# A two-layer feed-forward: weight sums behind the adds to h, squares and norm one job later, the last operand pair on VectorE

## The chip, the core and the metric

The kernel runs on one core of one Trainium2 chip. A core has a matrix engine (TensorE, "PE" in the profile), three engines for elementwise work (VectorE "DVE", ScalarE "ACT", GpSimd "POOL"), a queue that mainly issues transfers (SyncE "SP"), and DMA engines that move data between the device memory and the on-chip memory. Each engine runs its own instruction list in order and waits on semaphores for the others. The metric is the device time of one execution, in microseconds (us).

## The reference

The program computes two transformer blocks one after the other. The part that the change touches is the feed-forward of the second block, which occurs twice, once per layer:

```python
def _swiglu(h, w_gu, w_down):
    gate, up = jnp.split(h @ w_gu, 2, axis=-1)
    return (jax.nn.silu(gate) * up) @ w_down

for layer in range(DEPTH_2):              # 2 layers
    h = h + mixer(_rmsnorm(h, ...))       # even layer: recurrence and attention, odd: retention
    h = h + _swiglu(_rmsnorm(h, ffn_norm[layer]), ffn_w_gu[layer], ffn_w_down[layer])
```

`h` has 1024 features, held as eight tiles of 128 features (`hT`, index f). The norm divides each token by the root of the mean of its squared features. The kernel multiplies the raw, gain-scaled h by the weights and applies the norm's factor R to the product afterwards, so the products need not wait for the norm, but the silu does.

## The kernel before

**Numbers in two parts.** Every operand of a product is held as a high part (`whi`, `xo0`: a rounded copy, made by ScalarE) and a low part (`wlo`, `xo1`: the remainder, a subtraction on VectorE). One step of a product is three matmuls: high by high, high weights by low operand, low weights by high operand.

**Seven products per job.** The gate and up halves of one column tile of 128 are made together by a Strassen-Winograd scheme (class `Wino`). A "job" has seven products of four steps each (k = 0 to 3), `prod`, line 1853: A with `wa`, Bb with `w31`, C with `wa`, A with `w24`, the "fourth" product of the job before (`hhi`, `hlo`), Bb with `w24`, A with `w31`. A job thus has 28 steps; job 0 has no job before it and has 24. The letters A, Bb, C stand for banks of the matmul result memory; A alternates between banks 0 and 1, so job 2 writes the bank that job 0's A used.

**Weights.** `wa` is loaded as it is. `w31` is a sum of two blocks that the DMA engines form (a load by SyncE, then an accumulating load issued by GpSimd, line 1877). `w24` needs two additions on VectorE (lines 1913 and 1915, tile `s`) once that sum has landed. Each is then cast (`whi`) and subtracted (`wlo`, line 1891).

**Operands.** The mixer's last stage adds its output product to `hT` tile by tile in the order of `FORDER` (0, 4, 1, 5, 2, 6, 3, 7), lines 2533 and 2682. Behind each add, ScalarE scales the tile (`hid`, line 2167) and squares it (line 2172), GpSimd adds the square to a running sum (line 2173), and for each pair f, f+4 the seven operands j = 0 to 6 of step k are formed (`operands`): four differences `tt`, two on GpSimd (lines 1836, 1840) and two on VectorE (1838, 1841), and three splits into high and low parts (ScalarE line 296, VectorE line 299).

**Norm and result of a job.** In job 0, between A with `w24` and what follows, TensorE sums the squares over the partitions (line 2194), ScalarE takes the root, VectorE the reciprocal (line 2196). Then `put` finishes a job: GpSimd multiplies gate and up by R (2204), ScalarE takes silu (2206), GpSimd multiplies by R again (2208), VectorE multiplies gate and up, reading bank A (2212, 2213), and the product is split for the down product. `put` is a generator: `tick()` between the products advances the weights and the puts that are under way.

**What sets the order.** Up to job 0 a scheduler orders the instructions of each engine other than TensorE; from job 1 on `manual_schedule` keeps the order in which the code is written on all of them. `keep_in_program_order` pins one instruction, `issue_after` keeps what it holds behind a given instruction.

## Time and profile before

| what | value |
|---|---|
| median of 3 runs | 2330.43 us (2324.12 to 2332.87) |
| profiled execution | 2328.22 us |
| its span, first to last instruction | 2326.4 us |
| TensorE busy | 2164.4 us, 93% of the span |
| VectorE / ScalarE / GpSimd busy | 67% / 48% / 36% |
| job 0 of layer 0, with the norm's matmuls | 1149.86 to 1175.65 us |
| job 0 of layer 1, the same | 1962.86 to 1987.60 us |

The table is read as one execution: durations come from the profiled one, whose span lies 1.8 us below its own time. "Granted clock" (PEclk) is the share of TensorE's full speed that the chip allowed. Its two levels show as 1.00 and about half of that; a stretch in which both occur shows a number between them.

### The profile page before, as it was taken

The numbers are of one execution on the slowest core, as the hardware profiler recorded it, in microseconds if no ns is written. First come the engines' busy times: TensorE is split into PE (matmuls) and PEld (weight loads), VectorE is DVE, ScalarE is ACT, GpSimd is POOL, SyncE is SP. The second block draws the span as 40 slices with busy tenths as digits, with TensorE's granted clock in tenths as the row PEclk, the third lists the DMA queues.
The fourth block names the chain that finished last, engine by engine and source line by source line (L and its number), as shares of the span: only waits on it lengthen the run. The fifth ranks groups of instructions, "written<-read, shape, count | busy, mean of one in ns | idle before, by whom it ended". The sixth has DMA issues, their size and how long they took to land.

```text
span 2326.4 us, 34274 instructions
## 1 busy us (share of the span) xinstructions
PE 2164.4 (93%) x13208; PEld 1874.0 (81%) x13208; DVE 1561.5 (67%) x2146; ACT 1113.8 (48%) x1685; POOL 844.2 (36%) x564
## 2 busy tenths in 40 slices
PE   7789989987999988988899999999999998999999
PEld 1577768756777766877899999988888877999999
DVE  5764886547885876476897594665545556876864
ACT  4313654335876863656554352434323344544432
POOL 2325123234775653641444251422101213542522
PEclk9889989997999998988999999999999999999999
DMA  7564120485997861200366464322222224555642
GB/s 258 181 228 128 42 96 28 175 306 203 334 349 286 302 251 44 78 23 28 103 166 172 121 178 111 99 96 72 78 94 90 73 73 127 147 176 129 181 123 82
DMA packets 112544, 339.09 MB, mean 146 GB/s; under 512 B 14280, under 2 KB 17624, under 8 KB 112374
## 3 DMA queue, kind: packets, MB, share of 16 engines
q1 hardware_dynamic: 91168, 288.85, 36.4%
q0 software_dynamic: 11536, 31.75, 7.2%
q10 hardware_dynamic: 9670, 16.25, 2.2%
q8 instruction: 105, 1.72, 0.3%
q14 instruction: 65, 0.53, 0.1%
HBM read 326.18 MB, written 19.47 MB: 149 GB/s over the span
## 4 chain that ended last, share of the span: by engine, by line
PE 49%; DVE 6%; ACT 2%; issue 2%; POOL 2%; DMA 1%; DVEq 0%; POOLq 0%; ACTq 0%
PE p L1853 17%; PE p L1798 11%; PE p L2070 11%; PE p L2614 3%; PE p L2654 1%; DMA raw<-in_gu 1%; DVE wlo L299 1%; PE p L2617 1%; DVE xo L299 1%; DVE rv L2621 0%; PE p L2488 0%; POOL xt L1741 0%; PE gu L1637 0%; PE p L2458 0%; DVE wloF L1891 0%
## 5 line engine op out<-in xcount | busy, mean ns | idle before, releaser
L296 ACT CAST whi<-raw 128x1024 fp32r<-128x1024 f32 (+1 forms) x237 | 240.0, 1022 | 281.6 <-PE p L1798 120.0
L299 DVE TENSOR_TENSOR wlo<-raw,whi 128x1024 fp32r<-128x1024 f32 (+1 forms) x178 | 254.2, 1447 | 84.1 <-ACT whi L296 80.5
L1853 PE MATMUL p<-xo,whi 128*128 128x264 f32 (+1 forms) x1216 | 225.2, 284 | 18.6 <-ACT xo L296 8.7
L1798 PE MATMUL p<-x,whi 128*128 128x264 f32 (+1 forms) x992 | 230.1, 336 | 3.9 <-DVE xt L2343 1.9
L299 POOL TENSOR_TENSOR wlo<-raw,whi 128x1024 fp32r<-128x1024 f32 x59 | 153.7, 2612 | 189.6 <-ACT whi L296 161.6
L1853 PEld LDWEIGHTS p<-xo,whi 128*128 128x128 f32 x1216 | 188.5, 189 | 20.7 <-ACT xo L296 9.3
L1798 PEld LDWEIGHTS p<-x,whi 128*128 128x128 f32 x992 | 162.8, 194 | 26.1 <-issue 2.6
L1853 PE MATMUL p<-xo,wlo 128*128 128x264 f32 (+1 forms) x608 | 172.5, 284 | 1.2 <-DVE wlo L1891 1.2
L1853 PE MATMUL p<-xo,whiF 128*128 128x264 f32 (+1 forms) x896 | 170.8, 289 | 0.4 <-DVE hT L2682 0.4
L2070 PE MATMUL p<-hid,whi 128*128 128x264 f32 (+1 forms) x928 | 149.5, 283 | 0.0
L1798 PE MATMUL p<-x,wlo 128*128 128x264 f32 (+1 forms) x496 | 144.6, 336 | 0.9 <-DVE wlo L299 0.9
L1853 PEld LDWEIGHTS p<-xo,whiF 128*128 128x128 f32 x896 | 142.9, 194 | 1.1 <-DVE hT L2682 0.7
L1853 PE MATMUL p<-xo,wloF 128*128 128x264 f32 (+1 forms) x448 | 129.2, 288 | 0.0
L2070 PEld LDWEIGHTS p<-hid,whi 128*128 128x128 f32 x928 | 126.7, 188 | 0.2
L2080 DVE TENSOR_TENSOR hT<-hT,p 128x264 f32<-128x264 f32 (+1 forms) x96 | 36.5, 421 | 130.1 <-PE p L2070 130.1
L1360 PE MATMUL gu<-wlo,xh 128*128 128x512 f32 x272 | 110.6, 407 | 12.7 <-DVE wlo L299 7.4
L1853 PEld LDWEIGHTS p<-xo,wlo 128*128 128x128 f32 x608 | 115.1, 189 | 1.4 <-DVE wlo L1891 1.4
L1359 PE MATMUL gu<-whi,xh 128*128 128x512 f32 x272 | 112.1, 412 | 0.0
L1361 PE MATMUL gu<-whi,xlo 128*128 128x512 f32 x272 | 109.5, 402 | 1.8 <-DVE xlo L299 1.8
L1891 DVE TENSOR_TENSOR wlo<-raw,whi 128x1024 fp32r<-128x1024 f32 (+1 forms) x66 | 99.7, 1515 | 2.4 <-ACT whi L1927 1.0
L1798 PEld LDWEIGHTS p<-x,wlo 128*128 128x128 f32 x496 | 86.6, 193 | 10.2 <-issue 1.3
L2070 PE MATMUL p<-hid,wlo 128*128 128x264 f32 (+1 forms) x464 | 93.2, 282 | 0.0
(1317 smaller groups left out, 6044.8 us busy)
## 6 DMA issues: line engine op xcount, KB each, us to landing
raw<-in_moe SPq DMA_DIRECT2D x115, 512.0 KB, 6.1
raw<-in_gu SPq DMA_DIRECT2D x66, 512.0 KB, 4.6
sp<-in_moe SPq DMA_DIRECT2D x48, 512.0 KB, 6.4
raw<-in_gu POOLq DMA_DIRECT2D x44, 512.0 KB, 5.7
mixAB<-in_ada SPq DMA_DIRECT2D x32, 512.0 KB, 4.5
raw<-in_down SPq DMA_DIRECT2D x24, 512.0 KB, 5.9
rawF<-in_gu SPq DMA_DIRECT2D x22, 512.0 KB, 3.5
a<-in_gu SPq DMA_DIRECT2D x44, 256.0 KB, 2.7
```

The source lines that it names most:

```text
L296: i = nc.scalar.copy(hi, src)
L299: self.last = i, (lo_eng or nc.vector).tensor_tensor(lo, src, hi.bitcast(F32), op=ALU.subtract)
L1359: T_.matmul(acc, xh[:, k], hi[:, w], start=k == 0, stop=False)
L1360: T_.matmul(acc, xh[:, k], lo[:, w], start=False, stop=False)
L1361: T_.matmul(acc, xl[:, k], hi[:, w], start=False, stop=k == 7)
L1798: nc.tensor.matmul(a[:, :c1 - c0], w[wi][:, ks], x[xi][:, k, c0 - o:c1 - o], start=k == 0 and wi == 0 and xi == 0, stop=k == nk - 1 and wi ...
L1853: T_.matmul(bank[:, :W], w[wi][:, 512 * i + 128 * k:512 * i + 128 * k + 128], xo[xi][:, k, W * j:W * j + W], start=first and k == 0 and wi ...
L1891: lo = lambda w, src, n=1024: V.tensor_tensor(w[1][:, :n], src, w[0][:, :n].bitcast(F32), op=ALU.subtract)
L2070: nc.tensor.matmul(a_[:, :W], w[wi][:, ks], put.hid[xi][:, k, W * j:W * j + W], start=k == 0 and wi == 0 and xi == 0, stop=k == nk - 1 and ...
L2080: V.tensor_tensor(self.hT[:, f, c0:c1], self.hT[:, f, c0:c1], a_[:, :W], op=ALU.add)
L2614: T_.matmul(acc[t], x[xi][:, kk, ts_], w[wi][:, ws], start=kk == 0 and xi == 0 and wi == 0, stop=kk == 7 and xi == 1)
L2617: T_.matmul(acc[4][:96], xm[:, kk], w[wi][:, ws], start=kk == 0 and wi == 0, stop=kk == 7 and wi == 1)
```

## The change

Four things are edited. (1) In job 0, `w31` is made before `w24`; `w24`'s sums are issued behind the add of h tile f = 3, and job 1's `wa` and `w24` behind the last split of the operands. (2) The squares of the last six h tiles and their sums on GpSimd leave the operand stage and become a generator (`squares`) that the ticks of jobs 0 and 1 advance; the norm stands in job 1 rather than job 0, and job 0's `put` is started after it. (3) The two differences of the last pair that stood on GpSimd go to VectorE, and its four differences are split in two pieces. (4) Job 0 takes its first products in the order A, C, Bb, with bank 6 for C.

```diff
-    def operands(self, xg, f, xo):
+    def operands(self, xg, f, xo, near=False):
...
-        V, G = nc.vector, nc.gpsimd
+        V, G = nc.vector, nc.vector if near else nc.gpsimd
...
+        flat = tt.rearrange("p a n -> p (a n)")
+        if near:
+            b.split(part(0, 3, 5), part(1, 3, 5), flat[:, :2 * W])
         G.tensor_tensor(tt[:, 2], b22, b12, op=ALU.subtract)
         V.scalar_tensor_tensor(tt[:, 3], tt[:, 1], -1.0, b21, op0=ALU.mult, op1=ALU.subtract)
-        b.split(part(0, 3, 7), part(1, 3, 7), tt.rearrange("p a n -> p (a n)"))
+        n = 2 if near else 0
+        b.split(part(0, 3 + n, 7), part(1, 3 + n, 7), flat[:, n * W:])
...
-        lo = lambda w, src, n=1024: V.tensor_tensor(w[1][:, :n], src, w[0][:, :n].bitcast(F32), op=ALU.subtract)
+        lo = lambda w, src, n=1024: self.pin(V.tensor_tensor(w[1][:, :n], src, w[0][:, :n].bitcast(F32), op=ALU.subtract))
...
-            S_.copy(w[0], rs)
+            self.pin(S_.copy(w[0], rs))
...
-            w = self.pair()
-            yield w, s24_(w, ra, rs, i)
-            w = self.pair()
-            yield w, s31_(w, rs, i + 1)
+            s24, s31 = lambda w: s24_(w, ra, rs, i), lambda w: s31_(w, rs, i + 1)
+            for how in (s31, s24) if first else (s24, s31):
+                w = self.pair()
+                yield w, how(w)
+            first = False
...
-        self.make(3)
+        with B.tc.issue_after(B.added):
+            self.make(1)
+        with B.tc.issue_after(self.behind[0]), B.tc.issue_after(self.behind[1]):
+            self.make(2)
+        self.steps.append(self.squares)
         for i in range(2):
             self.half()
-        self.late = 5
+        self.late, self.pin = 5, B.tc.keep_in_program_order
...
-            wa, w24, w31 = have[:3]
-            A, Bb, C = self.A(), self.Bb(), self.C()
-            three = (A, wa, 0, 0), (Bb, w31, 1, 3), (C, wa, 1, 1)
+            A, Bb = self.A(), self.Bb()
             if i == 0:
-                for p_ in three:
-                    self.prod(*p_, ks=range(3))
+                wa, w31, w24 = have[:3]
+                C = B.bank(6)
+                three = (A, wa, 0, 0), (Bb, w31, 1, 3), (C, wa, 1, 1)
+                for p_ in (0, 2, 1):
+                    self.prod(*three[p_], ks=range(3))
+            else:
+                wa, w24, w31 = have[:3]
+                C = self.C()
+                three = (A, wa, 0, 0), (Bb, w31, 1, 3), (C, wa, 1, 1)
...
             self.prod(A, w24, 0, 4, False)
             add(g[:, 0], p1, C)
-            if i == 0:
+            if i == 1:
                 norm()
+                self.steps.append(first)
...
             pend = A, ready, u, p5
-            self.steps.append(put(g, u, A, ready))
+            p_ = put(g, u, A, ready)
+            if i:
+                self.steps.append(p_)
+            else:
+                first = p_
...
-        for f in FORDER:
-            hf = b.hT[:, f, o0:o0 + 2 * W]
-            S_.activation(xg[:, f], hf, AF.Copy, scale=gain[:, f:f + 1])
-            if f == 0:
-                S_.activation(a, hf, AF.Square)
-            else:
-                s = B.tmp(0)[:, :2 * W]
-                S_.activation(s, hf, AF.Square)
-                G.tensor_tensor(a, a, s, op=ALU.add)
+
+        def square(f, pin=False):
+            hf = b.hT[:, f, o0:o0 + 2 * W]
+            s = a if f == 0 else B.tmp(0)[:, :2 * W]
+            i = S_.activation(s, hf, AF.Square)
+            if pin:
+                tc.keep_in_program_order(i)
+            if f:
+                G.tensor_tensor(a, a, s, op=ALU.add)
+
+        def squares():
+            for f in FORDER[2:]:
+                square(f, True)
+                yield
+        for i, f in enumerate(FORDER):
+            S_.activation(xg[:, f], b.hT[:, f, o0:o0 + 2 * W], AF.Copy, scale=gain[:, f:f + 1])
             if f < 4:
-                gens[f] = wn.operands(xg, f, xo)
+                gens[f] = wn.operands(xg, f, xo, i == 6)
             next(gens[f % 4])
+            if i < 2:
+                square(f)
+        wn.behind = [i.ins for i in b.last]
+        wn.squares = squares()
...
 -                nc.vector.tensor_tensor(b.hT[:, f, a0:a1], b.hT[:, f, a0:a1], a[:, :a1 - a0], op=ALU.add)
+                i = nc.vector.tensor_tensor(b.hT[:, f, a0:a1], b.hT[:, f, a0:a1], a[:, :a1 - a0], op=ALU.add)
+            if f == FORDER[6]:
+                B.added = i.ins
```

The last hunk stands at the add to h in the first mixer; the second mixer's add (line 2682) is edited alike.

**VectorE, opening of layer 0's feed-forward.** The rows begin with the split of h tile 2 in both; `s` is the sum for `w24`, `wloF` with number 2583 belongs to `w24` before and to `w31` after; `hT` is the add to h (two pieces per tile). Before:

```order
L299 TENSOR_TENSOR xo_2575_11775<-hid_2573_11773,xo_2574_11774 128x264
L1913 TENSOR_TENSOR s_2584_11792<-raw_11778,rawF_11776 128x512
L1838 SCALAR_TENSOR_TENSOR tt_11845<-tt_11845,hid_2573_11773 128x264
L1915 TENSOR_TENSOR s_2584_11792<-s_2584_11792,rawF_11776 128x512
L1841 SCALAR_TENSOR_TENSOR tt_11845<-tt_11845,hid_2573_11773 128x264
L2533 TENSOR_TENSOR hT_9255<-hT_9255,p_2566_11705 128x264
L2533 TENSOR_TENSOR hT_9255<-hT_9255,p_2567_11706 128x264
L299 TENSOR_TENSOR xo_2575_11775<-hid_2573_11773,xo_2574_11774 128x528
L1891 TENSOR_TENSOR wlo_11886<-raw_11778,whi_11885 128x1024
L1891 TENSOR_TENSOR wloF_2583_11791<-s_2584_11792,whiF_2582_11790 128x1024
L2533 TENSOR_TENSOR hT_9255<-hT_9255,p_2571_11739 128x264
L2533 TENSOR_TENSOR hT_9255<-hT_9255,p_2572_11740 128x264
```

After:

```order
L299 TENSOR_TENSOR xo_2575_11775<-hid_2573_11773,xo_2574_11774 128x264
L2564 TENSOR_TENSOR hT_9255<-hT_9255,p_2561_11671 128x264
L2564 TENSOR_TENSOR hT_9255<-hT_9255,p_2562_11672 128x264
L1895 TENSOR_TENSOR wloF_2583_11791<-raw_11778,whiF_2582_11790 128x1024
L2564 TENSOR_TENSOR hT_9255<-hT_9255,p_2566_11705 128x264
L2564 TENSOR_TENSOR hT_9255<-hT_9255,p_2567_11706 128x264
L1838 SCALAR_TENSOR_TENSOR tt_11831<-tt_11831,hid_2573_11773 128x264
L299 TENSOR_TENSOR xo_2575_11775<-hid_2573_11773,xo_2574_11774 128x528
L1844 SCALAR_TENSOR_TENSOR tt_11831<-tt_11831,hid_2573_11773 128x264
L299 TENSOR_TENSOR xo_2575_11775<-hid_2573_11773,xo_2574_11774 128x264
L1836 TENSOR_TENSOR tt_11844<-hid_2573_11773 128x264
L2564 TENSOR_TENSOR hT_9255<-hT_9255,p_2571_11739 128x264
```

The two additions for `w24` and a low part have left the stretch, the low part of `w31` stands in front of the add of tile 3, and one difference of the last pair (L1836) has come to VectorE.

**ScalarE, end of job 0 and start of job 1 of layer 0.** `whi`/`whiF` are casts of weights (L1919 and L1923 `w24`, L1927 and L1931 `w31`), L2189 the moved squares, `xR` the roots. Before:

```order
L296 CAST xo_2574_11774<-tt_11864 128x1056
L1919 CAST whi_11896<-s_2606_11898 128x1024
L2099 COPY p_2614_11913<-p_2619_11918 128x264
L2102 COPY p_2615_11914<-p_2620_11919 128x264
L1927 CAST whiF_2622_11959<-raw_11782 128x1024
L2113 COPY u_2616_11915<-p_2619_11918 128x264
L2195 ACT_TABLE_LOAD
L2195 ACTIVATE xR_11884<-p_2624_11974,eps_60 128x264
L2195 ACTIVATE xR_11884<-p_2625_11975,eps_60 128x264
L1989 CAST hhi_11907<-a_2608_11905 128x512
L1989 CAST hhi_11911<-a_2611_11909 128x512
```

After:

```order
L2129 COPY u_2610_11899<-p_2613_11902 128x264
L1994 CAST hhi_11891<-a_2602_11889 128x512
L1923 CAST whi_11880<-s_2600_11882 128x1024
L2189 ACTIVATE xt_2616_11935<-hT_9255 128x528
L2189 ACTIVATE xt_2617_11942<-hT_9255 128x528
L1994 CAST hhi_11895<-a_2605_11893 128x512
L2189 ACTIVATE xt_2618_11949<-hT_9255 128x528
L2189 ACTIVATE xt_2621_11967<-hT_9255 128x528
L1931 CAST whiF_2619_11952<-raw_11782 128x1024
L2189 ACTIVATE xt_2622_11974<-hT_9255 128x528
L2189 ACTIVATE xt_2624_11992<-hT_9255 128x528
L1905 CAST whiF_2625_11997<-rawF_11869 128x1024
```

The cast of job 1's `w31` (`whiF` from `raw_11782`) now stands behind four of the moved squares. The tile `xt` that a square writes has two buffers, so the third and the fourth each wait for the sum two before it.

**VectorE, from the reciprocal to the first instruction that reads job 0's bank.** `rg` and `ru` are gate and up of a job, L2212 and L2243 the first instruction of `put` that reads bank A of job 0. Before, in job 0 and job 1:

```order
L2029 TENSOR_TENSOR rg__2617_11916<-p_2614_11913,p_2621_11920 128x264
L1891 TENSOR_TENSOR wloF_2623_11960<-raw_11782,whiF_2622_11959 128x1024
L2029 TENSOR_TENSOR rg__2617_11916<-u_2616_11915,p_2620_11919 128x264
L2196 RECIPROCAL xR_11884<-xR_11884 128x528
L2029 TENSOR_TENSOR ru__2618_11917<-p_2615_11914,p_2619_11918 128x264
L1913 TENSOR_TENSOR s_2639_12043<-raw_11889,rawF_11795 128x512
L1915 TENSOR_TENSOR s_2639_12043<-s_2639_12043,rawF_11795 128x512
L1891 TENSOR_TENSOR wloF_2628_12003<-rawF_11795,whiF_2627_12002 128x1024
L2029 TENSOR_TENSOR rg__2634_12025<-p_2631_12022,p_2638_12029 128x264
L1891 TENSOR_TENSOR wlo_12019<-s_2639_12043,whi_12018 128x1024
L2212 SCALAR_TENSOR_TENSOR ru__2618_11917<-p_2619_11918,rg__2617_11916 128x264
L2213 SCALAR_TENSOR_TENSOR ru__2618_11917<-ru__2618_11917,rg__2617_11916 128x264
```

After, in job 1 and the start of job 2:

```order
L2034 TENSOR_TENSOR ru__2612_11901<-p_2609_11898,p_2613_11902 128x264
L1917 TENSOR_TENSOR s_2637_12038<-raw_11871,rawF_11869 128x512
L1919 TENSOR_TENSOR s_2637_12038<-s_2637_12038,rawF_11869 128x512
L1895 TENSOR_TENSOR wloF_2620_11953<-raw_11782,whiF_2619_11952 128x1024
L1895 TENSOR_TENSOR wloF_2626_11998<-rawF_11869,whiF_2625_11997 128x1024
L2034 TENSOR_TENSOR rg__2632_12020<-p_2629_12017,p_2636_12024 128x264
L2227 RECIPROCAL xR_11863<-xR_11863 128x528
L1895 TENSOR_TENSOR wlo_12014<-s_2637_12038,whi_12013 128x1024
L1895 TENSOR_TENSOR wlo_12072<-raw_11871,whi_12071 128x1024
L2034 TENSOR_TENSOR rg__2632_12020<-u_2631_12019,p_2635_12023 128x264
L2243 SCALAR_TENSOR_TENSOR ru__2612_11901<-p_2613_11902,rg__2611_11900 128x264
L2244 SCALAR_TENSOR_TENSOR ru__2612_11901<-ru__2612_11901,rg__2611_11900 128x264
```

The reciprocal stands one job later, and with it the instruction that reads bank A of job 0; the first matmul of job 2, which writes that bank, waits for it in both kernels.

## Rows read from the trace of the kernel before

**Rows 1.** Page, part 1: busy time, share of the span and instructions per engine.
```profile
PE 2164.4 (93%) x13208; PEld 1874.0 (81%) x13208; DVE 1561.5 (67%) x2146; ACT 1113.8 (48%) x1685; POOL 844.2 (36%) x564
```

**Rows 2.** Windows: stretch, then busy time per engine, PEclk, DMA share.
```profile
1149.86:1175.65 25.79, 15.63 (x79) 13.97 (x77) 21.41 (x25) 15.24 (x22) 11.10 (x9) 0.74 0.55 150
1175.65:1185.87 10.22, 10.22 (x86) 10.22 (x85) 10.19 (x10) 5.60 (x9) 5.31 (x5) 1.00 0.38 82
...
1962.86:1987.60 24.74, 14.79 (x78) 13.34 (x76) 13.67 (x16) 11.64 (x19) 8.03 (x7) 0.66 0.43 113
1987.60:1997.50 9.90, 9.90 (x87) 9.90 (x86) 9.87 (x10) 5.23 (x9) 4.33 (x4) 1.00 0.31 56
```

**Rows 3.** Waits of TensorE, job 0 of layer 0: total, times, longest (us).
```profile
PE p L1853 <- ACT xo L296: 4.0, 1, 4.0
PE p L1853 <- ACT whiF L1919: 2.7, 1, 2.7
PE p L1853 <- DVE xo L299: 2.3, 2, 1.5
```

**Rows 4.** Timeline, TensorE, job 0 of layer 0: start, us, line, op, tiles.
```profile
1153.85 0.48 PE L1853 MATMUL p<-xo,whi 128*128 128x264 f32 x2 [2.72 <-ACT whiF L1919]
...
1169.20 0.65 PE L1853 MATMUL p<-xo,whiF 128*128 128x264 f32 x2
...
1171.18 1.71 PE L2194 MATMUL p<-xt,ones 128*128 128x264 f32 x4
...
1172.53 0.59 PE L1853 MATMUL p<-xo,whiF 128*128 128x264 f32 x2
```

**Rows 5.** Timeline, VectorE, around job 0 of layer 0.
```profile
1149.38 1.24 DVE L1913 TENSOR_TENSOR s<-raw,rawF 128x512 f32<-128x512 f32 x1
...
1152.95 0.76 DVE L2533 TENSOR_TENSOR hT<-hT,p 128x264 f32<-128x264 f32 x2
...
1155.38 1.21 DVE L1891 TENSOR_TENSOR wloF<-s,whiF 128x1024 fp32r<-128x1024 f32 x1
...
1160.73 3.03 DVE L1891 TENSOR_TENSOR wlo<-raw,whi 128x1024 fp32r<-128x1024 f32 x1
...
1165.97 1.25 DVE L299 TENSOR_TENSOR xo<-tt,xo 128x1056 fp32r<-128x1056 f32 x1
```

**Rows 6.** Timeline, GpSimd: a sum of squares beside a VectorE instruction.
```profile
1161.05 1.61 POOL L2173 TENSOR_TENSOR xt<-xt,xt 128x528 f32<-128x528 f32 x1
```

**Rows 7.** Source view of line 2173, the sums: count, ns min/median/max, span.
```profile
L2173 POOL TENSOR_TENSOR xt<-xt,xt x14: 1322/1498/2438, 1134.0 to 1975.0; 128x528 f32<-128x528 f32 x7, 128x512 f32<-128x512 f32 x7
```

**Rows 8.** Waits of TensorE, job 0 of layer 1.
```profile
PE p L1853 <- DVE xo L299: 4.8, 2, 4.1
PE p L1853 <- ACT xo L296: 4.7, 1, 4.7
```

**Rows 9.** Timeline, VectorE, layer 1: first sums of w24, job 0 and job 1.
```profile
1950.29 0.69 DVE L1913 TENSOR_TENSOR s<-raw,rawF 128x512 f32<-128x512 f32 x1 [3.21 <-DMA raw<-in_gu]
...
1967.17 0.69 DVE L1913 TENSOR_TENSOR s<-raw,raw 128x512 f32<-128x512 f32 x1 [7.07 <-DMA raw<-in_gu]
```

**Rows 10.** Timeline, ScalarE, layer 0: a square; then both square roots and job 0's silu.
```profile
1146.43 0.63 ACT L2172 ACTIVATE xt<-hT 128x528 f32<-128x528 f32 x1
...
1173.11 0.85 ACT L2195 ACTIVATE xR<-p,eps 128x264 f32<-128x264 f32 x2
...
1179.69 0.65 ACT L2206 ACTIVATE rg__2617_11916<-rg__2617_11916 128x528 f32<-128x528 f32 x1 [0.70 <-POOL rg__2617_11916 L2204]
```

**Rows 11.** Timeline, VectorE, layer 0: reciprocal; first instruction that frees job 0's bank.
```profile
1174.79 3.45 DVE L2196 RECIPROCAL xR<-xR 128x528 f32<-128x528 f32 x1
...
1184.61 0.42 DVE L2212 SCALAR_TENSOR_TENSOR ru__2618_11917<-p,rg__2617_11916 128x264 f32<-128x264 f32 x1
```

**Rows 12.** Timeline, GpSimd, layer 0: the two products with the norm's result.
```profile
1178.32 1.34 POOL L2204 TENSOR_TENSOR rg__2617_11916<-rg__2617_11916,xR 128x528 f32<-128x528 f32 x1 [1.23 <-DVE xR L2196]
...
1180.41 1.72 POOL L2208 TENSOR_TENSOR rg__2617_11916<-rg__2617_11916,xR 128x528 f32<-128x528 f32 x1 [0.75 <-ACT rg__2617_11916 L2206]
```

More of the change, by code (lines that the diff above doesn't have):

```diff
@@ L1931, in s31_ @@
             yield
-        i = 0
+        i, first = 0, True
         for job in jobs:
@@ L1999, in begin @@
         self.steps, self.halves, self.got, self.read, self.reads, self.summed = [], [], [], [], [], set()
-        self.have, self.pairs = [], []
+        self.have, self.pairs, self.pin = [], [], lambda i: i
         for job in jobs:
@@ L2052, in run @@
                 man.__enter__()
+                self.pin = lambda i: i
             if len(job.shape) == 2:
@@ L2532, in out @@
             for a, (a0, a1) in zip(B.lin(w, [m[:, 4 * o:4 * o + 4] for m in mix], HV, 4, acc=acc), HV):
-                nc.vector.tensor_tensor(b.hT[:, f, a0:a1], b.hT[:, f, a0:a1], a[:, :a1 - a0], op=ALU.add)
+                i = nc.vector.tensor_tensor(b.hT[:, f, a0:a1], b.hT[:, f, a0:a1], a[:, :a1 - a0], op=ALU.add)
+            if f == FORDER[6]:
+                B.added = i.ins
         for i, f in enumerate(FORDER):
@@ L2681, in mixer_ret @@
                 a = B.lin(w, (yh, yl), LV, o=16)[0]
-                V.tensor_tensor(b.hT[:, f, 16:], b.hT[:, f, 16:], a, op=ALU.add)
+                i = V.tensor_tensor(b.hT[:, f, 16:], b.hT[:, f, 16:], a, op=ALU.add)
+                if f == FORDER[6]:
+                    B.added = i.ins
         nxt.early()
```

## The prediction

> **What bounds the kernel now.** I read the page first: TensorE is busy for 93% of the span [rows 1], so what can be won is where it stands still. Then the windows around the two places that the diff touches: job 0 of the first feed-forward takes 25.79 us of which TensorE is busy for 15.63, at a granted clock of 0.74; job 1, with four steps more, takes 10.22 us at full clock, all of it busy [rows 2]. A full-clock step is therefore 10.22/28 = 0.365 us and job 0's 24 steps are worth 8.8 us. In layer 1 the figures are 24.74 us, 14.79 busy, clock 0.66, and 9.90/28 = 0.354 us, 8.5 us for 24 steps. With the norm's matmuls (1.35 us from the first of them to the next product [rows 4], taken alike for both layers) the two job 0s lose some 15.6 and 14.8 us. These 30 us are all that the change can reach. The waits say whose they are: in layer 0 4.0 us for the cast of the last four operands, 2.7 for the cast of `w24`, 2.3 for the low parts of operands, 9.0 us in all [rows 3]; most of the rest is slow clock. After the 2.72 us gap a step takes 0.66 us, as between the rows at 1169.20 and 1171.18, three steps [rows 4]. In layer 1 two waits of 4.8 and 4.7 us stand for operands [rows 8]. The row that matters most for layer 1 is the sum for job 1's `w24`, which sat on VectorE until its data landed at 1967.17, with a split of the operands behind it [rows 9].
>
> **Part 1, the operand stage of layer 0.** From the add of tile 3 (1152.95) to the end of the last split (1165.97 + 1.25 = 1167.2) VectorE takes 14.3 us [rows 5]. Out of the stretch go the 3.03 us low part of job 1's `wa` and one of its kind that took 1.21 (the one shown is the `wloF` at 1155.38), and that `wloF` itself, which moves ahead: 5.4 us. The splits and differences that were drawn out beside GpSimd's sums should lose some 1.5 us more; that is an estimate from the 3.03 against 1.21 us of the same operation [rows 5, 6]. In come two differences of 264 columns at 0.42 (as the instruction of that size at 1184.61 [rows 11]) and an extra piece of a split, 1.0 in all. That leaves 8.4 us. The start: the accumulated block was there when the first sum began, 1149.38 [rows 5], and one GpSimd sum less (1.5 us [rows 7]) stands before its issue, so it lands at 1148.0 to 1149.4. A cast and a 1.21 us low part later, 1150.3 to 1151.7, the stretch begins; the last split ends at 1158.7 to 1160.1, the low part of `w24` 1.2 us later. Twelve steps are left then. Eight at 0.66 and four at 0.365 make 6.7 us; all at half clock 7.9. Job 0 ends at 1166.6 to 1169.2; I take 1167.3. Before it was 1175.65 less the norm's 1.35, 1174.3. **Gain 7 us**, 5 to 7.7.
>
> **Part 2, job 1 of layer 0.** The squares begin where ScalarE has cast job 1's `w24`, by then about 1164; a square takes 0.63 [rows 10]. Six sums at the median 1.50 [rows 7] and one remainder of `hhi` between them, counted like a sum, are 10.5 us: the sums end at 1175.1 (1173.8 with the shortest, 1.32; 1181.7 if all took the longest, 2.44). Job 1's `w31` is queued on ScalarE behind four squares, the fourth of which waits for the second sum (1167.6): square and cast make 1169.3, the low part follows two additions on VectorE, 1170.5 to 1172.5. TensorE wants it four steps after job 0's end, 1168.8: a **new wait of 1.7 to 3.7 us**, I take 2.7. Twelve steps, partly at half clock (4.4 to 7.9, I take 6.7), lead to the norm, later than the sums; it ends at about 1179.6 (1176.5 to 1183).
>
> **Part 3, the norm's chain.** Behind the norm lie both roots 0.85, reciprocal 3.45, product 1.34, silu 0.65, product 1.72, and the 0.42 us that reads bank A of job 0 [rows 10 to 12]: 8.4 us. The profile before shows the same chain from the norm's end (1171.18 + 1.71 = 1172.9) to 1185.0, 12.1 us, since VectorE did other things between; these are the two bounds, and I take the lower, as the order after puts only two low parts, hidden beside GpSimd and ScalarE, between reciprocal and that instruction. Before, job 1's 28 steps hid it: job 2 started at 1185.87 [rows 2], 1.3 us after that instruction began. After, only twelve steps (4.4 us) stand between norm and job 2, so TensorE **waits 4.0 us** at bank A. Job 2 starts at 1179.6 + 8.4 = 1188.0, 2.1 us later than before; with the low ends 1184.9, with the high ones 1195. A wait of that length brought half clock before; eight steps at 0.66 instead of 0.365 cost 2.4 us, which job 2 then pays. **Layer 0: 4.5 us slower**, from 1 faster to 9 slower.
>
> **Part 4, layer 1.** Job 0's first accumulated block had landed by 1950.29, well ahead of the last add, so `w31` costs nothing there, and the sum at 1967.17 no longer stands in front of the operands [rows 9]. Without it the last pair is done some 4 us after the last product of the mixer (add, cast, three subtractions, two splits), at about 1967, and job 0's 24 steps end at 1972.5 to 1976.8 rather than 1986.2: a gain of 9.4 to 13.7. But the squares start only at about 1971.6. Six sums and two remainders at 1.5 last until 1983.4; `w31` of job 1 is ready at 1978.2 to 1979.5, a wait of about 4 us, and twelve steps and the norm (1.4) bring it to 1985 to 1987. Adding 8.4 gives job 2 at 1993.4 to 1995.4 (1999 with the 12.1 us chain) instead of 1997.5 [rows 2]: 2 to 4 us earlier; less 2.4 for the clock **1 us faster**, from 4 faster to 4 slower.
>
> **The remaining edits.** The order A, C, Bb and bank 6 cost nothing by themselves: C needs only the second piece of the operands, Bb the last. If `w31` came later than assumed they hide at most two steps, 0.7 us. From job 2 on the instruction lists of both kernels agree, but for `put` 0 in the first steps of job 2. VectorE is busy 10.19 of 10.22 us per job [rows 2], so it could not catch up on a backlog; it has none, since its low parts for job 2 are done during the wait.
>
> **A rule against the change.** Beside a GpSimd sum of 1.61 us a 1.21 us low part took 3.03 [rows 5, 6]. The Trainium skill says in "SBUF — State Buffer", section "SBUF: two separate sides", that VectorE with two on-chip inputs and GpSimd share a port pair as an exclusive lock, the one that comes second blocking for the whole instruction. By that rule the sums only change place and meet the additions and low parts of job 1 instead: two additions and one low part between the sums would put the norm about 2.6 us later in each layer, for 5 us more than the sum here; the trace agrees as to the one pair shown.
>
> **Sum.** 4.5 - 1 = 3.5 us on the span of 2326.4 us and on the profiled 2328.22 us: 2331.7. The median of the runs shown lies 2.2 us above the profiled one, so I predict 2334.
>
> **Rivals.**
> *The gain of job 0 stays* (faster). The roots and the reciprocal overlap with products, and job 1's `w31` is early: then 7 and 11.5 us remain, 2312 for the median. For it speaks that GpSimd has nothing but these sums there. Against it: the sums cannot end before 1173.8 in layer 0, and 1.35 + 8.4 us after that is 1183.6, a gain of 2.3 us at most; in layer 1 likewise about 7.
> *Squares and additions block one another* (slower). In job 1 GpSimd's sums meet VectorE's additions and low parts; at 2.44 instead of 1.50 [rows 7] six of them end 5.6 us later, and the chain behind takes 12.1 instead of 8.4. That decides once the sums end later than the product before the norm, at about 1178: then each layer pays 4 to 9 us more than in the sum, 2343 to 2350.
> *It doesn't open job 0* (nothing won). If the accumulated block lands late, the low part of `w31` now holds the adds of h behind it on VectorE. Each us late is a us on job 0, and the norm's chain follows: 3 us more, about 2337.
> *VectorE takes it all back.* Its 10.2 us of work per job is conserved, and a change that only moves it ends where it began: 2330.
>
> **How the numbers follow.** My forecast with the two rivals near it (2330, 2337) holds 0.62; the blocking rival 0.22; the kept gain 0.14; the rest, 0.02, falls on a larger slowdown. Half a per cent, 11.7 us, is about what a measurement of this kernel can tell from no change, which makes the bounds 2318.8 and 2342.1. Faster 0.14, same 0.62, slower 0.24. The forecast's own range is 2325 to 2343 from the ends above (1 and 4 faster, 9 and 4 slower); with the rivals it runs from 2315 to 2347.
>
> **What would show it.** In the profile after: job 0 of layer 0 at about 18 us up to its last step, no wait above 2.5 us in it; a wait of TensorE for `whiF` or `wloF` (L1931, L1895) four steps into job 1; the norm's matmuls some 12 us after job 0's end; a wait for VectorE's L2243 at job 2's first matmul, 4 us in each layer, and slow steps after it. No such wait would make the prediction wrong towards faster; job 2 at 1195 or later would make it wrong towards slower.

## The result, and the profile after

The changed kernel takes 2342.18 us (median of 8 runs, 2336.36 to 2346.5) against 2328.3 us for the kernel before on the same chips (8 runs). The ratio is 1.0064, with a 95% interval of 1.0047 to 1.0081: **13.9 us slower**. The profiled execution took 2344.39 us over a span of 2342.6.

Not all of the difference between the two profiled spans is the change's. An attention matmul that both kernels run ahead of the first edited instruction starts 2.55 us later in the changed one. First the kernel before, then the changed one (start, duration, engine, line):

```profile
1098.80 0.33 PE L2475 MATMUL p<-cst,pe 128*128 128x128 f32 x1 [0.27 <-DVE pe L2471]
```

```profile
1101.35 0.33 PE L2506 MATMUL p<-cst,pe 128*128 128x128 f32 x1 [0.26 <-DVE pe L2502]
```

So times of layer 0 are compared below after 2.55 us are taken off (called the old clock), or as lengths of stretches. The first windows to read are job 0, job 1 with the wait at its end, and job 2, of both layers (columns as in [rows 2]):

```profile
1151.26:1171.80 20.54, 14.46 (x75) 12.81 (x74) 15.15 (x26) 13.32 (x21) 5.49 (x6) 0.67 0.63 170
1171.80:1195.26 23.46, 14.32 (x90) 13.54 (x89) 16.85 (x13) 12.18 (x17) 15.39 (x10) 0.83 0.35 94
1195.26:1208.10 12.84, 12.84 (x84) 12.84 (x84) 10.66 (x13) 6.56 (x11) 4.51 (x5) 0.77 0.54 144
1975.04:1988.63 13.59, 10.51 (x74) 10.11 (x73) 10.66 (x18) 8.74 (x15) 1.50 (x2) 0.87 0.70 189
1988.63:2011.35 22.72, 13.66 (x90) 12.85 (x88) 14.95 (x13) 12.91 (x19) 17.39 (x12) 0.82 0.39 98
2011.35:2023.83 12.48, 12.48 (x84) 12.48 (x85) 10.55 (x13) 6.55 (x11) 4.49 (x5) 0.78 0.53 146
```

Job 0 did become shorter: 20.5 us against 24.4 without the norm's 1.35 in layer 0 [rows 2, 4], and 13.6 against 23.4 in layer 1. But job 1, which took 10.2 and 9.9 us at full clock, now takes 23.5 and 22.7, and job 2 runs at a granted clock of 0.77 and 0.78 and takes 2.7 and 2.6 us longer than before. (The third window ends with job 2's last matmul; job 3 begins at 1208.22.) From the end of the mixer to the start of job 3 that is 57.0 us instead of 46.3, and 48.8 instead of 44.5: 15.0 us lost. The mixer's end lies 1.15 us earlier relative to the attention matmul above (49.91 against 51.06 us to the first product), which leaves 13.8, the size of the measured difference. The waits of TensorE, first layer 0, then layer 1 (waited for: total, times, longest):

```profile
PE p L1857 <- DVE ru__2612_11901 L2243: 4.6, 1, 4.6
PE p L1857 <- ACT p L2114: 2.7, 1, 2.7
PE p L1857 <- DVE wloF L1895: 2.3, 1, 2.3
...
PE p L1857 <- ACT whiF L1931: 2.2, 1, 2.2
```

```profile
PE p L1857 <- DVE ru__3720_19505 L2243: 4.6, 1, 4.6
PE p L1857 <- ACT whiF L1931: 3.4, 1, 3.4
PE p L1857 <- DVE hT L2715: 3.1, 1, 3.1
PE p L1857 <- DVE wloF L1895: 1.1, 1, 1.1
```

The long waits for the last cast of operands and for job 1's data are gone [rows 3, 8]. Three others have come: for the cast and the low part of job 1's `w31`, together 4.5 us in each layer, for the copy of A that stands behind two casts on ScalarE (L2114), 2.7 us in layer 0, and for the instruction that reads bank A of job 0 (L2243), 4.6 us in each layer. In layer 1 job 0 also waits 3.1 us for the mixer's add to h (L2715), where that wait was 0.4 us before.

The copy of A and the wait for `w31` are both seen on ScalarE, at the end of job 0 and the start of job 1:

```profile
1162.36 1.04 ACT L1923 CAST whi<-s 128x1024 fp32r<-128x1024 f32 x1 [0.75 <-DVE s L1919]
1163.31 1.04 ACT L1905 CAST whi<-raw 128x1024 fp32r<-128x1024 f32 x1
1164.37 0.38 ACT L2114 COPY p<-p 128x264 f32<-128x264 f32 x1
...
1167.85 0.38 ACT L2129 COPY u<-p 128x264 f32<-128x264 f32 x1 [2.82 <-PE p L1857]
...
1168.65 1.04 ACT L1923 CAST whi<-s 128x1024 fp32r<-128x1024 f32 x1
1169.59 1.18 ACT L2189 ACTIVATE xt<-hT 128x528 f32<-128x528 f32 x2
...
1171.74 0.65 ACT L2189 ACTIVATE xt<-hT 128x528 f32<-128x528 f32 x1 [0.46 <-POOL xt L2193]
1174.00 0.64 ACT L2189 ACTIVATE xt<-hT 128x528 f32<-128x528 f32 x1 [1.62 <-POOL xt L2193]
1174.55 1.03 ACT L1931 CAST whiF<-raw 128x1024 fp32r<-128x1024 f32 x1
```

The copy of A (L2114) runs behind the casts of job 0's `w24` and job 1's `wa`. The first squares run at 1169.59, after a copy (L2129) that had to wait for a product of job 0 and a cast behind it. The third and fourth wait for sums on GpSimd, and the cast of `w31` (L1931) stands behind the fourth. The sums and the later products with the norm on GpSimd:

```profile
1170.38 3.59 POOL L2193 TENSOR_TENSOR xt<-xt,xt 128x528 f32<-128x528 f32 x2 [0.27 <-ACT xt L2189]
1173.93 1.72 POOL L1997 TENSOR_TENSOR hlo<-a,hhi 128x512 fp32r<-128x512 f32 x1
1175.61 6.79 POOL L2193 TENSOR_TENSOR xt<-xt,xt 128x528 f32<-128x528 f32 x4
...
1190.36 2.14 POOL L2235 TENSOR_TENSOR rg__2611_11900<-rg__2611_11900,xR 128x528 f32<-128x528 f32 x1 [6.81 <-DVE xR L2227]
1193.25 1.49 POOL L2239 TENSOR_TENSOR rg__2611_11900<-rg__2611_11900,xR 128x528 f32<-128x528 f32 x1 [0.75 <-ACT rg__2611_11900 L2237]
```

Six sums take 10.4 us, 1.73 each, where the median before was 1.50 [rows 7]. VectorE in the same stretch:

```profile
1166.66 0.68 DVE L1919 TENSOR_TENSOR s<-s,raw 128x512 f32<-128x512 f32 x1
...
1174.55 1.64 DVE L1919 TENSOR_TENSOR s<-s,rawF 128x512 f32<-128x512 f32 x1
1176.12 2.31 DVE L1895 TENSOR_TENSOR wloF<-raw,whiF 128x1024 fp32r<-128x1024 f32 x1
...
1186.82 3.45 DVE L2227 RECIPROCAL xR<-xR 128x528 f32<-128x528 f32 x1 [2.59 <-ACT xR L2226]
...
1194.77 0.43 DVE L2243 SCALAR_TENSOR_TENSOR ru__2612_11901<-p,rg__2611_11900 128x264 f32<-128x264 f32 x1 [0.85 <-POOL rg__2611_11900 L2239]
```

An addition that takes 0.68 alone takes 1.64 here, beside GpSimd's remainder of `hhi` (L1997), and a low part 2.31 instead of 1.21 [rows 5], beside GpSimd's sums. The four instructions of TensorE that carry the delay on:

```profile
1178.48 0.59 PE L1857 MATMUL p<-xo,wloF 128*128 128x264 f32 x1 [2.33 <-DVE wloF L1895]
...
1185.22 1.05 PE L2225 MATMUL p<-xt,ones 128*128 128x264 f32 x4
1185.91 0.61 PE L1857 MATMUL p<-xo,hhi 128*128 128x264 f32 x2
...
1195.26 0.81 PE L1857 MATMUL p<-xo,whiF 128*128 128x264 f32 x2 [4.59 <-DVE ru__2612_11901 L2243]
```

The low part holds TensorE until 1178.48, the norm's matmuls follow 6.7 us later, and from the next product at 1185.91 the chain of roots, reciprocal, products and silu takes 9.35 us to job 2's first matmul. The norm itself does not wait for the sums: they end at 1182.40 in layer 0, 2.8 us before its matmuls, and in layer 1 0.25 us before them.

### The profile page after: what moved, and what is told of

It is laid out like the page before. It is cut to its first block, busy times and chain, and to the rows that moved or that the text cites. A ratio compares the mean times of both kernels' runs of the same rounds, so it can differ in the third digit from the quotient of the medians.

```text
span 2342.6 us, 34273 instructions
## 1 busy us (share of the span) xinstructions
PE 2174.1 (93%) x13208; PEld 1880.3 (80%) x13208; DVE 1558.5 (67%) x2152; ACT 1117.7 (48%) x1687; POOL 845.6 (36%) x560
## 4 chain that ended last, share of the span: by engine, by line
PE 49%; DVE 6%; ACT 2%; POOL 2%; issue 1%; DMA 1%; DVEq 0%; POOLq 0%; ACTq 0%
PE p L1857 19%; PE p L2080 11%; PE p L1798 11%; PE p L2647 3%; PE p L2687 1%; DMA raw<-in_gu 1%; DVE wlo L299 1%; PE p L2650 1%; DVE rv L2654 0%; PE p L2519 0%; PE p L2489 0%; PE gu L1637 0%; PE p L2295 0%; POOL xt L1741 0%; DVE abm L299 0%
## 5 line engine op out<-in xcount | busy, mean ns | idle before, releaser
L2090 DVE TENSOR_TENSOR hT<-hT,p 128x264 f32<-128x264 f32 (+1 forms) x96 | 36.5, 421 | 130.1 <-PE p L2080 130.1
L1895 DVE TENSOR_TENSOR wlo<-raw,whi 128x1024 fp32r<-128x1024 f32 (+1 forms) x64 | 97.2, 1523 | 2.5 <-ACT whi L1931 1.0
L1881 POOL DMA_DIRECT2D raw<-in_gu x44 | 38.6, 878 | 164.4 <-DVE hT L2090 123.5
```

The source lines that it names most:

```text
L1881: nc.gpsimd.dma_start(r, src[1], accum_op=ALU.add)
L1895: lo = lambda w, src, n=1024: self.pin(V.tensor_tensor(w[1][:, :n], src, w[0][:, :n].bitcast(F32), op=ALU.subtract))
L2090: V.tensor_tensor(self.hT[:, f, c0:c1], self.hT[:, f, c0:c1], a_[:, :W], op=ALU.add)
```

## The experiments

All ten kernels are variants of the changed one or of the one before, each timed beside the kernel before on the same chip. The table gives their ratio to it, and from the profiled execution of each the time from the end of the mixer to the first matmul of job 1, 2 and 3 (us; layer 0 / layer 1). The last column sums the stretch to job 3 over both layers, less the 90.8 us of the kernel before. Stretches are used because the end of layer 0's mixer alone lay anywhere from 1142 to 1154 us in these executions, in no order that follows the edits. Medians of two variants are told apart here only where their intervals do not overlap.

| kernel | median, us | ratio to before (95%) | to job 1 | to job 2 | to job 3 | difference |
|---|---|---|---|---|---|---|
| before | 2328.3 | 1 | 25.8 / 24.7 | 36.0 / 34.6 | 46.3 / 44.5 | 0 |
| changed | 2342.2 | 1.0064 (1.0047 to 1.0081) | 20.5 / 13.6 | 44.0 / 36.3 | 57.0 / 48.8 | +15.0 |
| e1 | 2326.5 | 0.9997 (0.9984 to 1.0010) | 21.4 / 16.7 | 38.7 / 30.7 | 48.9 / 40.6 | -1.2 |
| e2 | 2338.6 | 1.0052 (1.0034 to 1.0069) | 19.4 / 13.5 | 41.9 / 36.0 | 54.8 / 48.6 | +12.6 |
| e3 | 2333.2 | 1.0025 (1.0010 to 1.0039) | 19.2 / 13.6 | 37.9 / 31.6 | 51.3 / 44.7 | +5.2 |
| e4 | 2334.2 | 1.0023 (1.0011 to 1.0036) | 20.5 / 13.7 | 40.4 / 33.4 | 53.5 / 45.7 | +8.4 |
| e5 | 2319.3 | 0.9959 (0.9945 to 0.9972) | 22.8 / 16.7 | 35.6 / 26.7 | 45.9 / 36.6 | -8.3 |
| e6 | 2325.9 | 0.9989 (0.9979 to 1.0000) | 23.5 / 24.2 | 33.7 / 34.1 | 44.0 / 43.9 | -2.8 |
| e7 | 2331.8 | 1.0016 (1.0007 to 1.0025) | 19.4 / 13.7 | 37.2 / 31.5 | 50.5 / 44.6 | +4.4 |
| e8 | 2336.5 | 1.0043 (1.0029 to 1.0056) | 22.5 / 20.5 | 40.2 / 37.2 | 53.3 / 49.3 | +11.8 |
| e9 | 2316.4 | 0.9955 (0.9938 to 0.9973) | 22.8 / 17.5 | 33.2 / 27.8 | 43.9 / 38.3 | -8.6 |
| e10 | 2342.5 | 1.0065 (1.0047 to 1.0083) | 20.5 / 13.6 | 44.9 / 36.5 | 57.4 / 48.7 | +15.3 |

My theory was the chain: the second edit lays the norm's chain bare at job 2's bank and puts job 1's `w31` behind the squares. Its rivals were that GpSimd's sums and VectorE hold each other up wherever the sums stand, and that VectorE's fixed work per job takes every gain back.

**e1: norm and squares back.**

```diff
-            if i < 2:
-                square(f)
+            square(f)
...
-        self.steps.append(self.squares)
...
-            if i == 1:
+            if i == 0:
                 norm()
-                self.steps.append(first)
...
-            p_ = put(g, u, A, ready)
-            if i:
-                self.steps.append(p_)
-            else:
-                first = p_
+            self.steps.append(put(g, u, A, ready))
```

> All eight squares with their sums are back in the operand stage and the norm and job 0's put are back in job 0; the other three edits stay. Chain theory (the loss is the norm's chain laid bare at job 2's bank and job 1's w31 queued behind the squares, both the work of this one edit): the chain is hidden again behind job 1's 28 steps, no wait for L1931/L1895 in job 1, and what w31-first wins in the two job 0s stays in part: 2316 to 2324 us. Contention theory (GpSimd's sums cost what they cost wherever they stand): job 0 is as long as in the kernel before and the time is that of before, 2328. VectorE theory (its work is conserved): 2328 too.

Measured 2326.45 us: 15.7 us less than the changed kernel, so the second edit carries the loss, and job 0 stays short (21.4 with the norm, 16.7). But the time is that of the kernel before, because TensorE still waited for job 1's `w31`, 2.0 us in layer 1 and in layer 0:

```profile
PE p L1857 <- DVE wloF L1895: 3.1, 1, 3.1
PE p L1857 <- ACT whiF L1931: 2.0, 1, 2.0
```

No square stood before it here. On VectorE the low part (L1895) stood behind the reciprocal (L2220):

```profile
1173.51 3.45 DVE L2220 RECIPROCAL xR<-xR 128x528 f32<-128x528 f32 x1
1176.88 1.16 DVE L1895 TENSOR_TENSOR wloF<-raw,whiF 128x1024 fp32r<-128x1024 f32 x1
```

Part of my theory was thus wrong: this wait is not the squares' alone. The pins hold `w31`'s cast and the low parts of job 0 to the order of the code; e5 takes them away. Both rivals had expected this time, the contention theory with a job 0 as long as before, which it was not; e5 tells the reasons apart.

**e2: `w31` before the squares that wait.**

```diff
+            for _ in range(4):
+                yield
             for f in FORDER[2:]:
                 square(f, True)
-                yield
+            yield
```

> The generator of squares waits four ticks and then issues all six, so that on ScalarE the cast of job 1's w31 stands behind two squares that wait for no sum, instead of behind four; nothing else moves but the remainders of hhi. Chain theory: the waits for L1931/L1895 in job 1 shrink from 4.5 us a layer to under 2.5, but in layer 1 the norm stood right behind the last sum, so the gain shows there only as far as the sums end earlier: 2 to 6 us less than the changed kernel, 2336 to 2340. Contention theory: 2342, as the sums are the same.

Measured 2338.55 us, 3.6 less, in the chain theory's range; but the interval overlaps that of the changed kernel, so the time alone does not decide. The waits do: that for the cast is gone, and that for the low part remains (2.6 and 3.0 us, a little over the 2.5 expected). In layer 1 the norm's matmuls (L2227) then wait for the last sum:

```profile
1992.71 1.13 PE L2227 MATMUL p<-xt,ones 128*128 128x256 f32 x4 [2.10 <-POOL xt L2193]
```

There the sums themselves are what the norm waits for, so in this layer a better order of the casts alone can give no more.

**e3: another bank for job 0's A.**

```diff
-            A, Bb = self.A(), self.Bb()
+            A, Bb = self.A() if i else B.bank(2), self.Bb()
```

> Job 0's product A takes bank 2 instead of bank 0, so job 1 takes bank 0, job 2 bank 1 and so on: the first matmul of job 2 no longer waits for job 0's put, job 3 is the first that waits for a put (job 1's). Chain theory: the 4.6 us wait and the slow steps behind it (2.4 us) go in both layers, 14 us less than the changed kernel, 2326 to 2331. VectorE theory: the work that VectorE did during that wait is late in jobs 2 and 3, and the wait comes back there as one for a low part or a put: 2336 to 2342.

Measured 2333.2 us, 9.0 less than the changed kernel; 14 were expected, and the time lies between the two ranges. The wait for L2243 is gone in both layers. The waits in layer 0 from job 1 to the start of job 3:

```profile
PE p L1857 <- ACT whiF L1931: 3.3, 1, 3.3
PE p L1857 <- DVE wloF L1895: 1.6, 1, 1.6
PE p L1857 <- DVE wlo L1895: 1.3, 1, 1.3
PE p L1857 <- ACT p L2114: 1.3, 1, 1.3
```

Two of 1.3 us each have come in job 2, for a low part and for a copy (1.4 and 1.3 in layer 1): of the 7.0 us a layer expected, some 2.6 were given back. VectorE's theory has that part right. Bank 2 also brought a wait of its own: in layer 0 job 0's first matmul waits 2.7 us for the mixer's add to h (L2564), which it does not in the changed kernel; yet job 1 starts 1.3 us sooner after the mixer's end than in the changed kernel, so this is not where the rest went. The bare chain thus costs about 9 us.

**e4: no sums.**

```diff
-            if f:
+            if f and not pin:
                 G.tensor_tensor(a, a, s, op=ALU.add)
```

> Leaves out the six moved sums on GpSimd (the squares stay, the norm is taken of two tiles instead of eight). Chain theory: job 1's w31 waits no longer on sums, so 3 to 4 us a layer go there and the norm comes as much earlier, but the chain behind the norm is as bare as before: 2332 to 2336. Contention theory: with the sums all of the loss goes, and the gain of the job 0s shows: 2318 to 2326.

Measured 2334.17 us, in the chain theory's range and above the contention theory's. The low part of `w31` takes its short time again (the addition ahead of it still took 1.66 us, beside GpSimd's remainder of `hhi`):

```profile
1176.06 1.21 DVE L1895 TENSOR_TENSOR wloF<-raw,whiF 128x1024 fp32r<-128x1024 f32 x1
```

The wait for L2243 stays at 4.6 us in both layers, and that for `w31` falls from 4.5 to 2.1 us in each; 3 to 4 us had been expected to go. All that the sums do in jobs 0 and 1, contention and queue together, costs 8 of the 13.9 us (15.0 - 8.4 = 6.6 by the stretches). Within the intervals that is as much as e3 won.

**e5: e1 without the pins.**

```diff
-        self.late, self.pin = 5, B.tc.keep_in_program_order
+        self.late = 5
```

> As e1 (squares in the operand stage, norm and put of job 0 in job 0), and the casts and low parts of w31 are left to the scheduler in job 0, so that job 1's w31 is cast ahead of the root and its low part ahead of the reciprocal. Chain theory (the only losses are the waits named in the traces): the waits of 5.2 and 2.0 us for job 1's w31 in e1 go, at most 1.2 us come back in each job 0 because that low part now stands before w24's: 2319 to 2323 us. VectorE theory (its work is conserved and the job 0s' gain is always given back): 2326 to 2328.

Measured 2319.32 us, at the low end of the chain theory's range. The waits for `w31` are gone, job 2 starts 3.1 and 4.1 us earlier than in e1, and the job 0s' gain is not given back: **0.9959 (0.9945 to 0.9972)** of the kernel before. VectorE's theory falls.

**e6: the third edit alone, on the kernel before** (`operands` as in the changed kernel).

```diff
-                gens[f] = wn.operands(xg, f, xo)
+                gens[f] = wn.operands(xg, f, xo, n_ == 6)
```

> The kernel before with one edit alone: the last pair's two differences on VectorE and its four differences in two pieces. If the operand stage gains by this edit, the 4.0 and 4.7 us waits for the last cast of operands become shorter: 2322 to 2326 us. If it gains by w31-first alone, nothing changes: 2327 to 2330.

Measured 2325.94 us, 0.9989 with an interval that ends at no change; the longest wait for the last operands became shorter, in layer 0 2.0 us where it was 4.0 [rows 3], in layer 1 3.9 where it was 4.7 [rows 8]. By the interval the edit is worth anything from nothing to 5 us.

**e7: e2 and e3 together.**

```diff
-            A, Bb = self.A(), self.Bb()
+            A, Bb = self.A() if i else B.bank(2), self.Bb()
...
+            for _ in range(4):
+                yield
             for f in FORDER[2:]:
                 square(f, True)
-                yield
+            yield
```

> The changed kernel with both edits of e2 and e3: bank 2 for job 0's A, and job 1's w31 cast behind two squares instead of four. If the two losses add up (9.0 and 3.6 us measured apart): 2329 to 2331 us. If the wait for the put moves to job 3 in full: 2333 to 2336.

Measured 2331.79 us, just above the sum of the two. Beside e3's bank an earlier `w31` brings only 1.4 us, which the intervals do not tell from nothing; in layer 1 job 2 starts 0.1 us earlier than in e3.

**e8: the second edit alone** (first, third and fourth undone, pins kept).

```diff
-        i, first = 0, True
+        i, first = 0, False
...
-        with B.tc.issue_after(B.added):
-            self.make(1)
-        with B.tc.issue_after(self.behind[0]), B.tc.issue_after(self.behind[1]):
-            self.make(2)
+        self.make(3)
...
-                gens[f] = wn.operands(xg, f, xo, i == 6)
+                gens[f] = wn.operands(xg, f, xo)
...
-                C = B.bank(6)
-                for p_ in (0, 2, 1):
-                    self.prod(*three[p_], ks=range(3))
+                for p_ in three:
+                    self.prod(*p_, ks=range(3))
```

> The kernel before with the second edit alone: squares of six tiles and norm in jobs 0 and 1, job 0's put after it; w24 first, last pair on GpSimd, order A, Bb, C. Chain theory: this edit is the whole loss, so with it alone the time is at least that of the changed kernel, 2340 to 2347 us. Contention theory: the operand stage gains the sums that leave it and the loss is smaller, 2330 to 2336.

Measured 2336.48 us, between the two ranges: 8.8 us slower than before. The interval just overlaps that of the changed kernel; the stretches say 11.8 against 15.0. The waits in layer 0 show why it is less:

```profile
PE p L1857 <- DVE ru__2612_11899 L2235: 4.9, 1, 4.9
...
PE p L1857 <- DVE wloF L1895: 0.7, 1, 0.7
```

The bare chain is there in full, 4.9 us, but job 1's `w31` is hardly late. Counted from the mixer's end, job 0 ends 2.0 us later than in the changed kernel, and `w31` is ready 2.0 us sooner, as the squares began 2.7 us sooner. What shortens job 0 thus exposes more of the loss behind it; but only about half of the difference is that. My expectation had counted the wait for `w31` as this edit's, wherever job 0 ends.

**e9: e5 with the last pair as before.**

```diff
-                gens[f] = wn.operands(xg, f, xo, i == 6)
+                gens[f] = wn.operands(xg, f, xo)
```

> As e5, but the last pair's two differences stand on GpSimd again and its four differences are split in one piece. Chain theory: e6 showed this edit alone worth 2.6 us on the kernel before; if the edits add up, this kernel takes 2321 to 2325 us. If w31-first needs the near pair (its low part stands before the adds of h, so the last pair is late either way): 2325 to 2328.

Measured 2316.4 us, **0.9955 (0.9938 to 0.9973)**, below both ranges and not to be told from e5. Beside the first edit the third shows no gain. This is the fastest kernel of the study, with e5. The window of job 1 in both layers:

```profile
1169.10:1179.57 10.47, 10.47 (x87) 10.31 (x85) 10.23 (x10) 6.36 (x11) 5.89 (x4) 1.00 0.30 96
1974.50:1984.73 10.23, 10.05 (x85) 9.85 (x84) 10.20 (x12) 6.43 (x10) 5.83 (x4) 1.00 0.46 148
```

Job 0, the norm included, takes 22.8 and 17.5 us where it took 25.8 and 24.7, and job 1 runs through at 10.5 and 10.2 us, at full clock.

**e10: the sums on VectorE.**

```diff
-                G.tensor_tensor(a, a, s, op=ALU.add)
+                (b.nc.vector if pin else G).tensor_tensor(a, a, s, op=ALU.add)
```

> The changed kernel with the six moved sums on VectorE instead of GpSimd: no work is left out, and in job 1 VectorE had 8 us without work. Queue theory (the squares stand before job 1's w31 and wait for the sums): sums of some 0.7 us end earlier, w31 comes with them, 3 us a layer: 2334 to 2338, as the chain behind the norm stays bare. Contention theory (GpSimd's sums stretch VectorE's low parts from 1.2 to 2.3 us): as without the sums, 2332 to 2335, and the low parts of job 1 take 1.2 us. VectorE theory: its queue becomes longer and the time stays at 2342 or rises.

Measured 2342.46 us: nothing won. Both the queue and the contention theory missed; the VectorE theory had expected this time. The wait of layer 0 for `w31`, beside that for L2243 of 4.6 us as before, and VectorE ahead of it:

```profile
PE p L1857 <- DVE wloF L1895: 6.5, 1, 6.5
```

```profile
1175.19 1.21 DVE L1895 TENSOR_TENSOR wloF<-rawF,whiF 128x1024 fp32r<-128x1024 f32 x1
1176.33 0.69 DVE L2193 TENSOR_TENSOR xt<-xt,xt 128x528 f32<-128x528 f32 x1
1176.95 1.21 DVE L1895 TENSOR_TENSOR wloF<-raw,whiF 128x1024 fp32r<-128x1024 f32 x1
```

Most sums take 0.69 us and the low parts 1.21, so that contention is gone. But five sums and the low part of job 2's `wa` (`wloF<-rawF`) now stand on VectorE before that of job 1's `w31`, and TensorE waits 6.5 us for it. The scheduler also swapped these two low parts in layer 0. In layer 1 it did not: five sums alone stand before the low part there, and TensorE waits 0.7 us for the cast and 4.7 for the low part, no less than with the sums on GpSimd (3.4 and 1.1). So a place behind the sums in VectorE's queue cost `w31` no less here than the sums on GpSimd had.

## Why the prediction held in sign and missed in size

The direction and the two new waits were right. The sum was not: 3.5 us forecast, 13.9 measured. That the range of 2325 to 2343 still holds 2342.2 owes something to luck. It stood on a median of three runs, 2330.4; with the 2328.3 of eight runs it would have ended at 2341. By the prediction's own half per cent the ratio of 1.0064 counts as slower, to which it had given 0.24. Two of its signs came out badly too: job 0 of layer 0 had a wait above 2.5 us, and job 2 began at 1195.26, past the 1195 named as too late (1192.7 on the old clock). Term by term:

1. **Part 1, job 0 of layer 0.** Forecast 7 us of gain, 5 to 7.7. Measured: job 1 starts at 1171.80, 1169.25 on the old clock, against 1174.3: 5 us, the low end; 1.15 of it is the mixer's. What the part missed is the copy of A (L2114) behind two casts on ScalarE, for which TensorE waited 2.7 us. Not all of that wait is the copy's: the low part of `w24` ended only at 1164.67, 0.14 us before TensorE went on, so without the copy less than 1 us would have been saved (an estimate from these two rows). The last split of the operands ended at 1160.3 on the old clock, where 1158.7 to 1160.1 was forecast.
2. **Part 4's job 0 of layer 1.** Forecast to end 9.6 to 13.9 us after its start, measured 13.6: inside, at the upper end.
3. **Part 2, the step that failed.** I let the squares begin once job 1's `w24` was cast, at 1164. On ScalarE that cast itself stands behind the copy of a product of job 0, and the first square ran at 1169.59 (1167.0 on the old clock), in layer 1 12.2 us after the start instead of 8.7. About 2 of these 3 us in layer 0 are item 1's: the squares move with the end of job 0, which the part did not allow for. With sums of 1.73 us and a low part of 2.31 the wait for `w31` came out at 4.5 us, not 2.7, and the norm ended at 1183.4 on the old clock where 1179.6 was forecast and 1183 the upper end. In layer 1 the wait was as forecast, 4.5 against about 4, but the sums ended 26 us after the start, not 20.5, and the norm came 3 to 5 us late.
4. **Part 3, the chain.** Forecast 8.4 us from the norm, measured 9.35 and 9.2: GpSimd's first product took 2.14 us instead of 1.34, beside a low part on VectorE that I had counted as hidden. The wait at job 2, 4.0 forecast, was 4.6 twice; e3 shows that this wait was worth what it cost less 2.6 us. The slow steps behind it cost 2.7 and 2.6, where 2.4 were forecast. One reading in this part was wrong without changing its sum: before, the chain of 12.1 us was hidden not by job 1's 28 steps (10.2 us) but by 36, the last eight of job 0 among them (1172.53 to 1185.87, 13.3 us).

Two more slips: the step of 0.66 us was read from rows that stand behind the 4.0 us wait for operands, not behind the 2.72 us gap (the size is right all the same), and layer 0's upper end of 9 leaves out the 2.4 us of slow steps.

Together: layer 0 10.7 us slower from the mixer's end to job 3 (forecast 4.5), layer 1 4.3 slower (forecast 1 faster). The excess over the forecast comes from late squares and slow sums in both layers; the mechanism was named, its size was put at a quarter of what it is. Of the rivals, the blocking one was nearest in time. (Its 4 to 9 us a layer on the forecast of 2334 make 2342 to 2352, not 2343 to 2350.) What was to decide for it, sums that end after the product before the norm, did not come, in layer 1 by 0.25 us: the delay went through `w31`. The Trainium skill's rule in "SBUF — State Buffer", section "SBUF: two separate sides", by which the sum would have been 5 us higher, was the better guide to the price: an addition and a low part beside GpSimd's additions took 1.64 and 2.31 us here, against 0.68 and 1.22 without them. But e10, where most of this meeting was gone and the time the same, shows that it alone does not set the time.

What stays open: how much of e4's 8 us is contention and how much is queue, as no run removed one without moving the other. Nor was the changed kernel run without its pins, so what they cost beside the moved squares is not shown.

## What to carry to other kernels

Before you move a chain one stage later, look for the buffer that its last instruction frees, and count the work that is left between the chain's start and that buffer's next use; here 36 steps had hidden a chain that 12 could not. When work leaves a crowded stage, follow every queue it joins: the squares were cheap where they ran, and dear because the next job's weights stood behind them on ScalarE and VectorE. An edit that shortens one stage is best timed apart from the one that pays for it: the first and fourth edits, without the pins and with the norm where it was, took some 0.4% off the kernel (e9); the whole change made it 0.6% slower.

## What the runs showed of the hardware

TensorE's rate fell not only after one long wait. In job 0 of layer 0 of the changed kernel it had waited 0.9 and then 1.2 us and run on for 0.9 us, when a matmul with a low part of the weights (`wloF`) took 0.39 us, where those before it had taken 0.28. The first matmul after the next wait, of 0.2 us, took 0.59, where the first after each of the earlier two waits had taken 0.39, as TensorE's timeline of that stretch shows:

```profile
1155.77 0.39 PE L1857 MATMUL p<-xo,whiF 128*128 128x264 f32 x1 [1.21 <-DVE xo L299]
...
1156.71 0.39 PE L1857 MATMUL p<-xo,wloF 128*128 128x264 f32 x1
1157.27 0.59 PE L1857 MATMUL p<-xo,whiF 128*128 128x264 f32 x1 [0.17 <-ACT xo L296]
```

That is the step from the upper of the clock's two levels (2.4 GHz) to the lower (1.2): the granted clock was 1.00 up to 1156.73 and 0.50 after it. After the 4.6 us waits job 2 showed a granted clock of 0.77 and 0.78 and took 2.7 and 2.6 us more than before; in layer 0 its first eight steps took 5.45 us, where eight at full clock take 2.9.
